# A 31-tap depthwise convolution: four taps in one stationary tile of 32 columns

## The chip, the core and the metric

The kernel runs on one core of a Trainium2 chip. The metric is the time of one execution on the device in microseconds (us); each number below is from one of three timed runs or from one execution taken by the hardware profiler. TensorE (PE) does the matmuls, VectorE (DVE), ScalarE (ACT) and GpSimd (POOL) the elementwise work, and SyncE's queue (SP) issues nearly all DMA transfers, in order.

## The reference

The reference is a two-layer transformer over 1024 latent and 256 context tokens with 1024 channels, in fp32. The change is in layer 0, a Conformer convolution module:

```python
u = h @ w_pw1 + b_pw1
a, g = jnp.split(u, 2, axis=-1)
v = a * jax.nn.sigmoid(g)
v = dwconv(v, w_dw, b_dw)          # 31 taps along the tokens, each channel with its own weights
v = jax.nn.silu(layernorm(v, ln_g, ln_b))
return v @ w_pw2 + b_pw2
```

After it come a gated feed-forward layer, a layer of windowed attention and a second feed-forward layer, which take most of the time and are not touched.

## The kernel before

Channels lie on the 128 partitions, in eight chunks; tokens lie along the free dimension. For chunk c the gated product fills a row `v` of 1325 columns: 512 + 512 latent and 256 context tokens, with 15 zeros before, between and after. The convolution makes 1295 output columns from it, each a sum over 31 shifted reads of `v`.

The eight chunks are computed in rounds (the loop over c in the block under `manual_schedule`). There the order on PE, DVE, ACT and POOL is that of the code; the SP queue's order is set by a scheduler. In round c the convolution of chunk c runs beside the first product of chunk c+1. Each weight is split into two parts, so `glu_mm` does 24 matmuls for one half (gate or value) of one of three token tiles, 0 and 1 of 512 columns, 2 of 256. Its two PSUM tiles rotate (`s`, two buffers). `glu_out` applies the sigmoid on ACT and writes its part of `v` on DVE. Beside that, `ada_steps` computes a block of modulation values in four parts on PE, each with its own 512 KB of weights, loaded through the two buffers `raw`, which the weights of the product (`wh`, `wl`) pass through as well.

The 31 taps of a chunk are shared out by `NPE` and `NDV` (L816, L817): in chunks 0 to 5, TensorE takes 2 (`tap_steps`: a diagonal 128x128 stationary matrix for each tap, then three copies by ACT and one addition by POOL), DVE takes 18, multiplying and adding into an accumulator `cacc` that lies in PSUM (`dve`), and ACT and POOL take 11 together: ACT multiplies (`first` and `prod`), POOL adds into `a2`. Chunk 6 has 4, 17 and 10, chunk 7 has 10, 14 and 7. At the end of a chunk `last` adds both accumulators into `y`, and `ymean` sums `y` over channels on TensorE. Chunk 7 has no next product beside it; the layer norm follows it.

## Time and profile before

| what | value |
| --- | --- |
| three timed runs | 2763.06, 2765.3 (median), 2769.14 us |
| the profiled execution: time, span | 2764.74 us, 2762.8 us |
| busy share of the span: PE, DVE, ACT, POOL | 96%, 62%, 37%, 22% |
| mean granted TensorE clock | 0.991 of full speed |

The span runs from the first to the last instruction; the profiled execution's own time is 1.94 us longer than it. A share of the whole span says little of one stage. The convolution and what prepares it take the first 400 us; the rounds run from about 82 to 399 us.

### The profile page before, as it was taken

The page shows a single profiled execution, that of the slowest core. Times are in us where ns is not written, and L with a number is a line of the kernel's source. Part 1 is how long each engine was busy: PE and PEld are TensorE (multiplying, and loading weights), DVE is VectorE, ACT ScalarE, POOL GpSimd, SP SyncE. Part 2 cuts the span into 40 slices and gives each one's busy share as a digit, 9 for nine tenths or more (in the row PEclk, how much of TensorE's full clock was granted, in tenths as well). Part 3 has the DMA queues.
Part 4 walks back from the last instruction along what each step waited for, and adds up shares of the span by engine and source line. Part 5 has one row for each costly group of instructions (what it writes and reads, how often), then busy time and mean ns, then how long its engine had stood idle before and what let it go on. Part 6 is the DMA issues. An engine that isn't in the chain of part 4 may idle for free.

```text
span 2762.8 us, 32879 instructions
## 1 busy us (share of the span) xinstructions
PE 2654.9 (96%) x13280; PEld 2151.3 (78%) x13280; DVE 1707.3 (62%) x2325; ACT 1011.8 (37%) x1430; POOL 613.0 (22%) x423
## 2 busy tenths in 40 slices
PE   5999989999999999999999998999999999999997
PEld 3766645778888888888887887888878888888886
DVE  6899965554454554454547758999865545555546
ACT  5554535552111122111123427777652222222223
POOL 1788853320000000000003205566420000000003
PEclk9999999999999999999999999999999999999998
DMA  6222355321111111111111451232111111111111
GB/s 234 69 77 84 103 199 186 114 78 68 39 38 39 39 39 39 38 39 39 39 39 46 151 183 45 73 81 53 39 54 50 50 46 49 51 46 46 52 48 69
DMA packets 62759, 198.23 MB, mean 72 GB/s; under 512 B 7696, under 2 KB 13456, under 8 KB 60304
## 3 DMA queue, kind: packets, MB, share of 16 engines
q1 hardware_dynamic: 62608, 196.14, 20.9%
q8 instruction: 104, 1.70, 0.3%
q14 instruction: 47, 0.39, 0.0%
HBM read 180.38 MB, written 15.73 MB: 71 GB/s over the span
## 4 chain that ended last, share of the span: by engine, by line
PE 78%; DVE 12%; ACT 5%; issue 2%; POOL 1%; DMA 1%; SPq 0%; DVEq 0%; ACTq 0%; POOLq 0%
PE up_ps L186 38%; PE dn_ps L186 18%; PE glu_ps L186 4%; DVE cacc L740 3%; PE wo_ps L186 3%; PE pw_ps L186 2%; PE pB L186 2%; PE pA L186 2%; PE tp L1419 1%; DVE tl L175 1%; DVE wl L128 1%; PE v_ps L186 1%; PE ada_ps L204 1%; PE dn_tail L186 1%; DVE mx L1397 1%
## 5 line engine op out<-in xcount | busy, mean ns | idle before, releaser
L128 DVE TENSOR_TENSOR wl<-raw,wh 128x1024 fp32r<-128x1024 f32 x181 | 237.7, 1317 | 515.9 <-issue 312.1
L186 PE MATMUL up_ps<-x_l,wh 128*128 128x512 f32 (+1 forms) x1760 | 415.0, 370 | 4.2 <-POOL x_l L315 4.2
L186 PE MATMUL up_ps<-x_h,wl 128*128 128x512 f32 (+1 forms) x1760 | 409.7, 369 | 0.2 <-ACT x_h L304 0.2
L186 PE MATMUL up_ps<-x_h,wh 128*128 128x512 f32 (+1 forms) x1760 | 407.9, 369 | 0.0
L250 POOL TENSOR_TENSOR acc<-acc,scrh 128x256 f32<-128x256 f32 (+1 forms) x36 | 37.4, 1039 | 1575.2 <-ACT scrh L249 1573.3
L186 PEld LDWEIGHTS up_ps<-x_l,wh 128*128 128x128 f32 x1760 | 311.9, 189 | 64.2 <-POOL x_l L315 5.8
L186 PEld LDWEIGHTS up_ps<-x_h,wh 128*128 128x128 f32 x1760 | 311.4, 189 | 55.8 <-issue 0.8
L186 PEld LDWEIGHTS up_ps<-x_h,wl 128*128 128x128 f32 x1760 | 310.5, 189 | 56.2 <-issue 0.8
L454 DVE SCALAR_TENSOR_TENSOR y<-dn_ps,mods,y 128x512 f32<-128x512 f32 (+1 forms) x400 | 270.3, 694 | 129.1 <-PE dn_ps L186 129.0
L126 ACT CAST wh<-raw 128x1024 fp32r<-128x1024 f32 x194 | 201.9, 1042 | 358.2 <-PE dn_ps L186 328.1
L409 ACT ACTIVATE c<-up_ps,pv 128x1282 f32<-128x1282 f32 (+1 forms) x88 | 115.6, 1315 | 588.3 <-PE up_ps L186 588.3
L746 POOL TENSOR_TENSOR a<-a,pr 128x1295 f32<-128x1295 f32 x75 | 223.9, 2985 | 60.6 <-ACT pr L745 50.7
L186 PE MATMUL dn_ps<-gl,wh 128*128 128x512 f32 (+1 forms) x800 | 232.7, 372 | 0.7 <-DVE y L454 0.7
L186 PE MATMUL dn_ps<-gh,wl 128*128 128x512 f32 (+1 forms) x800 | 231.5, 371 | 0.0
L186 PE MATMUL dn_ps<-gh,wh 128*128 128x512 f32 (+1 forms) x800 | 231.0, 370 | 0.0
L740 DVE SCALAR_TENSOR_TENSOR cacc<-v,pv,cacc 128x1295 f32<-128x1295 f32 x131 | 205.7, 1570 | 4.0
L1413 POOL TENSOR_TENSOR p<-p,rd 128x640 f32<-128x640 f32 (+1 forms) x128 | 154.4, 1237 | 234.1 <-DVE rd L1411 164.9
L413 DVE SCALAR_TENSOR_TENSOR c<-up_ps,pv,c 128x1281 f32<-128x1281 f32 (+1 forms) x88 | 124.6, 1416 | 121.6 <-ACT c L409 121.6
L186 PEld LDWEIGHTS dn_ps<-gl,wh 128*128 128x128 f32 x800 | 142.7, 188 | 31.7 <-DVE y L454 6.5
L186 PEld LDWEIGHTS dn_ps<-gh,wh 128*128 128x128 f32 x800 | 145.1, 188 | 27.1
L186 PEld LDWEIGHTS dn_ps<-gh,wl 128*128 128x128 f32 x800 | 145.0, 188 | 26.9
L745 ACT ACTIVATE pr<-v,pv 128x1295 f32<-128x1295 f32 x75 | 102.9, 1377 | 73.5 <-POOL a L746 58.6
(252 smaller groups left out, 4088.4 us busy)
## 6 DMA issues: line engine op xcount, KB each, us to landing
raw<-in_up_dram SPq DMA_DIRECT2D x88, 512.0 KB, 3.5
ada<-in_adaw_dram SPq DMA_DIRECT2D x11, 2048.0 KB, 8.5
raw<-in_down_dram SPq DMA_DIRECT2D x44, 512.0 KB, 3.5
raw<-in_adaw_dram SPq DMA_DIRECT2D x38, 512.0 KB, 3.9
raw<-in_pw_dram SPq DMA_DIRECT2D x32, 512.0 KB, 3.6
qs<-q_dram SPq DMA_DIRECT2D x32, 256.0 KB, 5.3
raw<-in_wo_dram SPq DMA_DIRECT2D x16, 512.0 KB, 3.5
ada<-in_adaw_dram SPq DMA_DIRECT2D x7, 1024.0 KB, 13.6
```

Of the source, the lines that this page charges most:

```text
L126: nc.scalar.copy(out=wh, in_=raw)
L128: lo_engine[0].tensor_sub(out=wl, in0=raw, in1=wh)
L175: (leng or nc.vector).tensor_sub(out=l_out, in0=src, in1=h_out)
L186: nc.tensor.matmul(ps, lhsT=w, rhs=x, start=first and n == 0, stop=last and n == len(seq) - 1)
L250: (eng or nc.gpsimd).tensor_add(out=acc, in0=acc, in1=sq)
L409: nc.scalar.activation(out=c, in_=ps[:, :W], func=AF.Identity, bias=seg("fdb", l * 2 * NJ + ab * NJ + j, 1), scale=wd[1])
L413: nc.vector.scalar_tensor_tensor(out=c[:, 1:W], in0=ps[:, 0:W - 1], scalar=wd[0], in1=c[:, 1:W], op0=ALU.mult, op1=ALU.add)
L454: nc.vector.scalar_tensor_tensor(out=h, in0=ps[:, m * n:(m + 1) * n], scalar=mod(l, 5, dc, s), in1=h, op0=ALU.mult, op1=ALU.add)
L740: nc.vector.scalar_tensor_tensor(out=r.acc, in0=v[:, j:j + OW], scalar=tap(j), in1=r.acc, op0=ALU.mult, op1=ALU.add)
L745: nc.scalar.activation(out=pr, in_=v[:, j:j + OW], func=AF.Copy, scale=tap(j))
L746: nc.gpsimd.tensor_tensor(out=r.a2, in0=r.a2, in1=pr, op=ALU.add)
L1413: nc.gpsimd.tensor_tensor(out=it.p4[:, hh, :it.wid], in0=it.p4[:, hh, :it.wid], in1=rd[:, hh:hh + 1].to_broadcast([P, it.wid]), op=ALU.mult)
```

## The change

TensorE's taps in a chunk become 8 (chunks 0 to 5), 16 and 28, those of DVE 13, 8 and 0, those of ACT and POOL 10, 7 and 3. One stationary tile now holds four taps of 32 channels: its 128 rows are four copies of these channels' `v`, each copy shifted by m columns against the one before (m is a quarter of TensorE's taps), and its 32 columns are the 32 channels. Four such tiles beside each other, g = 0 to 3, cover the 128 channels and write the four quarters of the partitions. With m steps along the columns that gives 4m taps. The matmuls write `cacc` itself, and DVE adds its taps onto it; the copies by ACT and the addition by POOL of the old path are gone.

The shifted copies are made by DMA: `Shifted.load(t)` issues 16 transfers from `v` (4 shifts by 4 groups, 32 partitions each), once for each token tile, 48 in a chunk. In front of the rounds the code creates `Shifted(0, ...)` and calls `load(0)` twice. The weights are brought in by 16 small transfers (`load_taps`) into the buffer `vp`, which the shifted copies use afterwards, and are put in order by 32 copies on ACT (`pack_taps`). `a2` has one buffer instead of two. The parts of the modulation block and the product's weights are loaded at other places, and the matmuls of token tile 2 take `wl` first.

The diff, cut to its core (the lines that it removes are those of `tap_diags`, `tap_steps` and the old loop above):

```diff
+NPE = (8, 8, 8, 8, 8, 8, 16, 28)
+NDV = (13, 13, 13, 13, 13, 13, 8, 0)
...
+    def mm3(ps, ops, by_chunk=False, first=True, last=True, wl_first=False):
+        if wl_first:
+            seq = [(wl, xh) for wh, wl, xh, xl in ops]
+            seq += [(wh, xl) for wh, wl, xh, xl in ops]
+            seq += [(wh, xh) for wh, wl, xh, xl in ops]
...
+        id4 = cv.tile([P, 32], F32, name="id4", bufs=1)
+        nc.vector.tensor_reduce(out=id4, in_=ident.rearrange("p (r m) -> p m r", m=32),
+                                axis=AX.X, op=ALU.add)
+        wpk = cv.tile([P, SUM_M, 4], F32, name="wpk", bufs=1)
+        def load_taps():
+            o, n = SEG["wdw"]
+            w = cv.tile([P, 4, n], F32, tag="vp", name="wdw4", bufs=1)
+            for r in range(4):
+                for g in range(4):
+                    nc.sync.dma_start(out=w[32 * r:32 * r + 32, g],
+                                      in_=par[32 * g:32 * g + 32, o:o + n])
+            return w
+        def pack_taps(w):
+            for r in range(4):
+                rows = slice(32 * r, 32 * r + 32)
+                for c in range(KC):
+                    m = NPE[c] // 4
+                    o = sum(NPE[:c]) // 4
+                    nc.scalar.copy(
+                        out=wpk[rows, o:o + m, :],
+                        in_=w[rows, :, c * TAPS + m * r:c * TAPS + m * r + m].rearrange("p g s -> p s g"))
...
+        M = [n // 4 for n in NPE]
+        MO = [sum(M[:c]) for c in range(KC)]
+        def tap_weights(c):
+            m = M[c]
+            if m * P <= 256:
+                w = cv.tile([P, 256], F32, tag="dg", name="dg", bufs=1)
+            else:
+                w = cv.tile([P, OW], F32, tag="pr", name="dg", bufs=2)
+            w = w[:, :m * P]
+            nc.gpsimd.tensor_tensor(
+                out=w.rearrange("p (g m) -> p g m", m=32),
+                in0=id4.unsqueeze(1).to_broadcast([P, 4 * m, 32]),
+                in1=wpk[:, MO[c]:MO[c] + m, :].rearrange("p s g -> p (s g)").unsqueeze(2).to_broadcast([P, 4 * m, 32]),
+                op=ALU.mult)
+            return w
+        class Shifted:
+            def __init__(self, c, v):
+                self.v, self.m = v, M[c]
+                self.sp = OW + self.m - 1 - 512
+                self.a = cv.tile([P, 4, OW - 512 + 12], F32, tag="vp", name="vp", bufs=1)
+                self.b = [nt.tile([P, 512], F32, tag=("acc", "acc", "nt", "nt")[g], name="vpb",
+                                  bufs=(2, 2, 3, 3)[g]) for g in range(4)]
+            def copy(self, dst, c0, c1):
+                for r in range(4):
+                    for g in range(4):
+                        x0 = self.m * r + c0
+                        nc.sync.dma_start(out=dst(g)[32 * r:32 * r + 32],
+                                          in_=self.v[32 * g:32 * g + 32, x0:x0 + c1 - c0])
+            def load(self, t):
+                e = self.sp + self.m - 1
+                f = min(512, PADW + 512 - 3 * self.m)
+                if t == 0:
+                    self.copy(lambda g: self.a[:, g, 0:f], 0, f)
+                elif t == 1:
+                    self.copy(lambda g: self.a[:, g, f:e], f, e)
+                else:
+                    self.copy(lambda g: self.b[g], self.sp, self.sp + 512)
+            def rows(self, g, s, o, n):
+                if o < self.sp:
+                    return self.a[:, g, o + s:o + s + n]
+                return self.b[g][:, o - self.sp + s:o - self.sp + s + n]
+        def pe_taps(c, vp, w):
+            r = {}
+            sp = vp.sp
+            def part(o, e):
+                if o == 0:
+                    r["acc"] = pc.tile([P, 1536], F32, tag="cv", name="cacc")[:, :OW]
+                for s in range(vp.m):
+                    for g in range(4):
+                        nc.tensor.matmul(r["acc"][32 * g:32 * g + 32, o:e],
+                                         lhsT=w[:, (4 * s + g) * 32:(4 * s + g + 1) * 32],
+                                         rhs=vp.rows(g, s, o, e - o), start=s == 0,
+                                         stop=s == vp.m - 1)
+            return r, [lambda o=o, e=e: part(o, e)
+                       for o, e in ((0, 512), (512, sp), (sp, 1024), (1024, OW))]
+        def conv_steps(c, v, r, npe, ndve):
...
+                r["a2"] = cv.tile([P, OW], F32, tag="a2", name="a2", bufs=1)
+                nc.scalar.activation(out=r["a2"], in_=v[:, npe + ndve:npe + ndve + OW],
+                                     func=AF.Identity, bias=seg("bdw", c, 1), scale=tap(npe + ndve))
...
+                nc.gpsimd.tensor_tensor(out=r["a2"], in0=r["a2"], in1=pr, op=ALU.add)
...
+            dq = [lambda j=j: dve(j) for j in range(npe, npe + ndve)]
...
+            w4 = load_taps()
...
             apply(1, 0, 2)
             glu_out(q, 0)
+            vp = Shifted(0, q.v)
+            vp.load(0)
             apply(1, 2, 4)
             bcast_b(2)
+            pack_taps(w4)
+            dgs = tap_weights(0)
+            vp = Shifted(0, q.v)
+            vp.load(0)
             glu_mm(q, 1, 0, 0)
             normalize_h(2)
...
             glu_mm(q, 1, 1, 1)
             glu_out(q, 1)
+            vp.load(1)
             glu_mm(q, 2, 0)
             glu_mm(q, 2, 1)
             glu_out(q, 2)
+            vp.load(2)
...
+            ld_ada(0, 0)
+            ld_ada(0, 1)
             for c in range(KC):
+                wide_taps = M[c] * P > 256
+                if wide_taps:
+                    dgs = tap_weights(c)
+                r, taps = pe_taps(c, vp, dgs)
+                first, pq, dq, last = conv_steps(c, q.v, r, NPE[c], NDV[c])
                 ada_ps = pc.tile([P, 512], F32, tag="s", name="ada_ps", bufs=2) if c == KC - 1 else None
+                ada = ada_steps(0, 4 + c, lambda u, c=c: araw[c, u], ada_ps)
                 first()
                 run(pq, 1)
                 if c + 1 < KC:
                     q = glu_begin(c + 1)
                     glu_mm(q, 0, 0)
                     run(ada, 1)
+                    ld_ada(c, 2)
+                    run(pq, 0 if wide_taps else 1)
+                    glu_mm(q, 0, 1)
+                    run(ada, 1)
+                    ld_ada(c, 3)
+                    run(taps, 4)
+                    glu_out(q, 0)
+                    vp = Shifted(c + 1, q.v)
+                    vp.load(0)
+                    run(pq, 1)
                     if c > 0:
                         ymean(c - 1)
+                    glu_mm(q, 1, 0)
                     run(ada, 1)
+                    w_load()
+                    run(dq, 3)
                     run(pq, 2)
+                    run(ada, 1)
+                    w_load()
+                    glu_mm(q, 1, 1)
+                    run(ada, 1)
                     run(dq, 3)
                     run(pq, 1)
                     glu_out(q, 1)
+                    vp.load(1)
+                    if M[c + 1] * P <= 256:
+                        dgs = tap_weights(c + 1)
+                    wh = w_hi()
                     glu_mm(q, 2, 0)
                     run(ada, 1)
+                    run(dq, 2)
+                    run(pq, 1)
+                    w_lo(wh)
+                    ld_ada(c + 1, 0)
+                    wh = w_hi()
                     glu_mm(q, 2, 1)
                     run(dq, 1)
                     glu_out(q, 2)
+                    vp.load(2)
+                    w_lo(wh)
+                    ld_ada(c + 1, 1)
                     run(pq, 99)
                     run(dq, 99)
                 else:
+                    run(ada, 1)
+                    ld_ada(c, 2)
+                    run(ada, 1)
+                    ld_ada(c, 3)
+                    run(pq, 99)
                     ymean(c - 1)
+                    run(taps, 2)
                     run(ada, 2)
+                    run(taps, 1)
+                    run(ada, 1)
+                    for i in range(4):
+                        load_ada(i)
+                    run(taps, 1)
+                    run(dq, 99)
                 last()
```

On the SP queue, this is what stood between the last loads ahead of the rounds and the second round (`raw` from `in_adaw` is a part of the modulation block, from `in_pw` a weight of the product):

```order
L626 DMA ada_128<-in_adaw_dram 128x2048 x2
L599 DMA h_112<-in_hT_dram 128x8x256
L106 DMA raw<-in_pw_dram 128x1024 x2
L106 DMA raw<-in_adaw_dram 128x1024 x4
L106 DMA raw<-in_pw_dram 128x1024 x2
L106 DMA raw<-in_adaw_dram 128x1024 x4
```

In its place there stands, from the tap weights to the second round:

```order
L631 DMA wdw_244<-in_par_dram 32x248 x16
L109 DMA raw<-in_pw_dram 128x1024 x2
L778 DMA vp<-v 32x512 x32
L778 DMA vp<-v 32x273 x16
L778 DMA vpb<-v 32x512 x16
L109 DMA raw<-in_adaw_dram 128x1024 x4
L778 DMA vp<-v 32x512 x16
L109 DMA raw<-in_pw_dram 128x1024 x2
L778 DMA vp<-v 32x273 x16
L109 DMA raw<-in_adaw_dram 128x1024
L778 DMA vpb<-v 32x512 x16
L109 DMA raw<-in_adaw_dram 128x1024 x3
```

Between the loads of `raw` now stand bursts of 16 transfers; the first part of a modulation block is behind the second burst of a chunk, the second part behind the third (`vpb`).

On PE, from the last matmuls of chunk 0's product, through the taps of round 0 (`tap_ps`), to the first part of the modulation block (`glu_ps` is the product of the next chunk):

```order
L186 MATMUL glu_ps<-xh_508,wh 128x256 x8
L756 MATMUL tap_ps<-v,dg 128x512 x4
L756 MATMUL tap_ps<-v,dg 128x271 x2
L186 MATMUL glu_ps<-xl_242,wh 128x512 x8
L186 MATMUL glu_ps<-xh_241,wl 128x512 x8
L186 MATMUL glu_ps<-xh_241,wh 128x512 x8
L204 MATMUL ada_ps<-raw,c_80 32x512 x2
```

and now, from the start of round 0's product to the end of its taps (`cacc`):

```order
L193 MATMUL glu_ps<-xl_262,wh 128x512 x8
L193 MATMUL glu_ps<-xh_261,wl 128x512 x8
L193 MATMUL glu_ps<-xh_261,wh 128x512 x8
L211 MATMUL ada_ps<-raw,c_80 32x512 x2
L193 MATMUL glu_ps<-xl_262,wh 128x512 x8
L193 MATMUL glu_ps<-xh_261,wl 128x512 x8
L193 MATMUL glu_ps<-xh_261,wh 128x512 x8
L211 MATMUL ada_ps<-raw,c_80 32x512 x2
L806 MATMUL cacc<-vp,dg 32x512 x8
L806 MATMUL cacc<-vp,dg 32x272 x8
L806 MATMUL cacc<-vpb,dg 32x240 x8
L806 MATMUL cacc<-vpb,dg 32x271 x8
```

The taps have moved from ahead of the round's product to behind its first token tile and the second part of the modulation block; 6 matmuls of 128 columns each have become 32 of 32 columns.

## Rows read from the trace of the kernel before

**Rows 1.** The page, part 1: busy us, share of the span, instructions.

```profile
PE 2654.9 (96%) x13280; PEld 2151.3 (78%) x13280; DVE 1707.3 (62%) x2325; ACT 1011.8 (37%) x1430; POOL 613.0 (22%) x423
```

**Rows 2.** Stretches of two rounds: length, busy us by engine, clock, DMA share, GB/s.

```profile
126.15:166.00 39.85, 35.54 (x173) 25.31 (x172) 39.25 (x32) 18.93 (x19) 32.94 (x16) 0.98 0.28 91
166.00:207.00 41.00, 40.56 (x195) 29.62 (x194) 35.75 (x26) 21.86 (x22) 35.30 (x18) 0.98 0.20 67
```

**Rows 3.** The timeline of DVE: start, us, instruction, idle before and its releaser.

```profile
112.59 0.75 DVE L709 SCALAR_TENSOR_TENSOR v<-glu_ps,pv,sg 128x512 f32<-128x512 f32 x1 [3.26 <-PE glu_ps L186]
...
118.78 0.48 DVE L709 SCALAR_TENSOR_TENSOR v<-glu_ps,pv,sg 128x256 f32<-128x256 f32 x1 [0.57 <-PE glu_ps L186]
...
322.38 0.47 DVE L709 SCALAR_TENSOR_TENSOR v<-glu_ps,pv,sg 128x256 f32<-128x256 f32 x1
...
361.51 0.48 DVE L709 SCALAR_TENSOR_TENSOR v<-glu_ps,pv,sg 128x256 f32<-128x256 f32 x1 [1.57 <-PE glu_ps L186]
...
397.10 1.62 DVE L767 TENSOR_TENSOR y<-cacc,a 128x512 f32<-128x512 f32 x3 [8.81 <-POOL a L761]
```

**Rows 4.** The timeline of PE in round 0, same columns.

```profile
81.74 3.60 PE L756 MATMUL tap_ps<-v,dg 128*128 128x512 f32 x8
...
86.66 2.21 PE L186 MATMUL glu_ps<-xl,wh 128*128 128x512 f32 x8
...
92.44 1.05 PE L204 MATMUL ada_ps<-raw,c 128*32 128x512 f32 x4
93.42 2.12 PE L186 MATMUL glu_ps<-xl,wh 128*128 128x512 f32 x8
...
106.74 2.12 PE L186 MATMUL glu_ps<-xl,wh 128*128 128x512 f32 x8
...
112.32 1.11 PE L186 MATMUL glu_ps<-xl,wh 128*128 128x256 f32 x8
...
118.51 3.60 PE L756 MATMUL tap_ps<-v,dg 128*128 128x512 f32 x8
```

**Rows 5.** The tile cacc: instructions, ns min/median/max, first and last start.

```profile
L740 DVE SCALAR_TENSOR_TENSOR cacc<-v,pv,cacc x131: 1558/1572/1574, 86.3 to 386.7; 128x1295 f32<-128x1295 f32 x131
L767 DVE TENSOR_TENSOR y<-cacc,a x24: 406/675/691, 126.1 to 398.3; 128x512 f32<-128x512 f32 x16, 128x256 f32<-128x256 f32 x8
```

**Rows 6.** The tile pr: the additions on POOL, same columns.

```profile
L746 POOL TENSOR_TENSOR a<-a,pr x75: 2924/2995/3041, 85.4 to 391.1; 128x1295 f32<-128x1295 f32 x75
```

**Rows 7.** The timeline of PE: a modulation block ahead of the rounds.

```profile
31.71 2.00 PE L204 MATMUL ada_ps<-ada,c 128*32 128x512 f32 x16
```

**Rows 8.** The timeline of ACT, and of PE (last row), ahead of the rounds.

```profile
3.71 0.22 ACT L86 ACTIVATE c<-ctile 128x16 f32<-128x16 f32 x1
...
64.17 1.51 ACT L665 ACTIVATE xh<-h,mods,amul 128x512 fp32r<-128x512 f32 x2
...
75.17 0.66 ACT L707 ACTIVATE sg<-glu_ps,pv 128x512 f32<-128x512 f32 x1
...
75.89 1.21 PE L186 MATMUL glu_ps<-xl,wh 128*128 128x256 f32 x8 [0.53 <-ACT sg L707]
```

**Rows 9.** The timeline of SP in the attention layer: issues of small transfers.

```profile
1609.39 0.42 SPq L1320 DMA_DIRECT2D ks<-k_dram  x1
...
1612.64 0.42 SPq L1319 DMA_DIRECT2D ks<-k_dram  x1
```

**Rows 10.** The page, part 6: DMA issues, KB each, median us to landing.

```profile
raw<-in_adaw_dram SPq DMA_DIRECT2D x38, 512.0 KB, 3.9
...
ks<-k_dram SPq DMA_DIRECT2D x32, 112.0 KB, 4.5
ks<-k_dram SPq DMA_DIRECT2D x32, 80.0 KB, 2.2
```

**Rows 11.** The timeline of PE after a wait ahead of the rounds.

```profile
41.44 1.12 PE L216 MATMUL ada_pt<-ident,ada_sb 128*128 128x128 f32 x4 [7.74 <-ACT ada_sb L210]
...
43.21 0.63 PE L186 MATMUL glu_ps<-xh,wh 128*128 128x512 f32 x1
43.63 0.63 PE L186 MATMUL glu_ps<-xh,wl 128*128 128x512 f32 x1
```

More of the change, by code (lines that the diff above doesn't have):

```diff
@@ L34 @@
 DEPTH = 2
+NPE = (8, 8, 8, 8, 8, 8, 16, 28)
+NDV = (13, 13, 13, 13, 13, 13, 8, 0)
+SUM_M = sum(NPE) // 4
 SEGS = [
@@ L701, in glu_mm @@
                 ops = ops[4 * part:4 * part + 4]
-            mm3(q.ps[half][:, :n], ops, part is not None, part in (None, 0), part in (None, 1))
+            mm3(q.ps[half][:, :n], ops, part is not None, part in (None, 0), part in (None, 1),
+                t == 2)
         def glu_out(q, t):
@@ L765, in last @@
             def last():
                 for t, (o, n) in enumerate(TOK):
[L767 to L768 removed]
+                    nc.vector.tensor_tensor(out=ys[t][:, c, :], in0=r["acc"][:, OOF[t]:OOF[t] + n],
+                                            in1=r["a2"][:, OOF[t]:OOF[t] + n], op=ALU.add)
             pq = [lambda j=j: prod(j) for j in range(npe + ndve + 1, TAPS)]
[L771 removed]
@@ L772, in conv_steps @@
-            return first, tap_steps, pq, dq, last
+            dq = [lambda j=j: dve(j) for j in range(npe, npe + ndve)]
+            return first, pq, dq, last
         def ymean(c):
@@ L870, in hybrid_dit_kernel, with ld_ada, w_load, w_hi @@
             ys = [make_h(t, "y") for t in range(3)]
-            for c in range(KC):
-                first, tap_steps, pq, dq, last = conv_steps(c, q.v, dgs, NPE[c], NDV[c])
+            araw = {}
+            wraw = []
+            def ld_ada(c, u):
+                if c < KC:
+                    araw[c, u] = load_raw(adaw[0, 4 + c, :, 2 * u:2 * u + 2, :])
+            def w_load():
+                wraw.append(load_raw(queue[len(loaded) + len(wraw)][1]))
+            def w_hi():
+                wh = wpool.tile([P, 1024], F32R, tag="wh", name="wh", bufs=3)
+                nc.scalar.copy(out=wh, in_=wraw[0])
+                return wh
+            def w_lo(wh):
+                wl = wpool.tile([P, 1024], F32R, tag="wl", name="wl")
+                nc.vector.tensor_sub(out=wl, in0=wraw.pop(0), in1=wh)
+                loaded.append((wh, wl))
+            ld_ada(0, 0)
+            ld_ada(0, 1)
+            for c in range(KC):
+                wide_taps = M[c] * P > 256
[3 more added lines that the diff above has]
+                first, pq, dq, last = conv_steps(c, q.v, r, NPE[c], NDV[c])
                 ada_ps = pc.tile([P, 512], F32, tag="s", name="ada_ps", bufs=2) if c == KC - 1 else None
-                ada = ada_steps(0, 4 + c, None, ada_ps)
+                ada = ada_steps(0, 4 + c, lambda u, c=c: araw[c, u], ada_ps)
                 first()
-                run(dq, 1)
                 run(pq, 1)
                 if c + 1 < KC:
-                    parts, add = tap_steps("pr")
-                    for f in parts:
-                        f()()
-                    add()
                     q = glu_begin(c + 1)
@@ L931, in hybrid_dit_kernel @@
-                    assert not pq and not dq
-                    for f in evs:
-                        f()
-                    add()
+                    run(taps, 1)
[4 more added lines that the diff above has]
+                    run(dq, 99)
                 last()
```

72 lines of the change are left out of this document (4 added, 68 removed).

## The prediction

> **What bounds the kernel now.** I read the page's busy table first, then stretches of the rounds, then DVE's and PE's timelines in one round. TensorE is busy for 96% of the span [rows 1], but the change touches only the convolution, so the stage decides. In two successive rounds, of 39.85 and 41.00 us, DVE is busy for 39.25 and 35.75 us and PE for 35.54 and 40.56 us [rows 2]: neither has room, and the end passes from one to the other. A round is read between the writes of the last third of `v`: 118.78 to 322.38 is five rounds, 40.7 us each; round 6 takes 39.1 us (to 361.51); chunk 7 ends with its `y` at 398.72, 37.2 us later, 8.8 us of which DVE waited for POOL [rows 3].
>
> Within round 0, PE's taps take 4.9 us (81.74 to 86.66) and the product and the modulation block 31.85 us (86.66 to 118.51); a half product of 512 columns takes 5.8 us, a part of the modulation block 0.98 us (92.44 to 93.42), and from the end of token tile 1 to the end of tile 2 it is 6.2 us (112.32 to 118.51) [rows 4]. Ahead of the rounds ACT is in one chain: token tile 2's product waits at 75.89 for the sigmoid that ACT starts at 75.17, behind all its normalising work [rows 8].
>
> **The change, part by part.**
>
> *DVE and POOL.* DVE loses five of 18 taps of 1.57 us, 7.9 us a round; 13 remain, 20.4 us, and the sums into `y` (1.76 us) [rows 5]. With the writes of `v` (0.75, 0.75 and 0.48 us [rows 3]) DVE has 24.2 us a round beside the weight splits. POOL keeps nine additions of 3.0 us, 27 us [rows 6]. So neither bounds a round near 40 us any more. `a2` has one buffer, so ACT's next `first` waits for `last`, and the sigmoid of tile 0 stands behind it; both are done before TensorE needs that PSUM tile, behind the taps. If that cover went, each us would be a us of the round.
>
> *TensorE's taps.* An fp32 matmul is two instructions in the trace (the 8 instructions at 81.74 are 4 matmuls in the order). A modulation block ahead of the rounds, 8 matmuls of 512 columns that go to four column groups in turn, takes 2.00 us [rows 7], so four beside each other take 1.00 us. That is the shape of the new taps. Two steps of 1295 columns come to 2 x 1295 / 1024 x 2.00 = 5.1 us, against 4.9 before: eight taps for the price of two. With m = 4 it is 10.1 us, with m = 7 17.7 us. The bounds: nothing below this, since column groups are all that overlaps here; above, four times as long if they did not overlap. I take the row, since its shape is the same. The Trainium skill ("TensorE: Matmul & The Clock Gate", Measured speedup vs the span model) gives less for packing: 3.07 times for four tiles. From the 0.9 us of a matmul at 81.74 that would be an estimated 1.17 us for four instead of 1.00 and put about 10 us on the sum; the row of this kernel is faster than the page.
>
> A round of TensorE without waits is then 31.85 + 5.1 + about 1.0 for the three column means (like one part of the block) = 37.9 us, less than the 40.7 us of now.
>
> *The bursts on SP.* Each chunk adds 48 transfers to one queue. Small transfers on 32 partitions were issued seven in 3.25 us, 0.464 us apart [rows 9], so a burst of 16 takes 7.4 us. No row has a transfer from SBUF to SBUF; the nearest are those of 80 KB, which land in 2.2 us, against 4.5 us for 112 KB; a `raw` of 512 KB takes 3.9 us [rows 10]. Lower bound of a burst: 16 issues at 0.41 us (the issue alone, without the gap) = 6.6 us. Upper: eight in flight that take 4.5 us to land, 9.0 us. I take 7.4, the pitch of the same kind of transfer.
>
> In a round the second and third burst stand ahead of the modulation block's first two loads, which the PE order needs behind the product's halves for tile 0. From the end of tile 1's product (0): `v` is written 1.0 us later (112.32 to 113.34 [rows 3, 4]), the burst ends at 8.4, part 0 lands at 12.3, where PE needs it at 6.2 + 5.8 = 12.0. The next burst runs from 8.9 to 16.3; its `v` is there in time, after PE's 6.2 and some 2 us of DVE. Part 1 lands at 20.2, PE needs it at 12.0 + 1.0 + 5.6 (a half as at 106.74 to 112.32) = 18.6. So PE waits 1.6 us, and the round is 37.9 + 1.6 = 39.5 us: five rounds save 5 x 1.2 = 6 us. Round 6 has 5.1 us of taps more, 44.6 against 39.1: it loses 5.5 us. In chunk 7 no product lies in between: part 1 lands 14.0 us behind the end of its product (20.2 - 6.2), then follow 1.0 + 1.0 + 10.8 of taps (789 of 1295 columns) + 1.0 + 6.9 + 1.8 of sums = 36.5 us against 37.5: a gain of 1 us, though POOL's wait of 8.8 us is gone.
>
> *Ahead of the rounds.* `pack_taps` puts 32 copies into ACT's chain. The shortest ACT row with few columns takes 0.22 us [rows 8]; I take 0.2 us, 6.4 us in all (bounds: 0 if they overlap wholly, 7.0 at 0.22). The chain holds PE, so the rounds start 6.4 us late, at 88.1 instead of 81.74. The shifted copies use the buffer of the packed weights, so the first burst starts behind the copies, at 64.2 + 6.4 = 70.6. `load(0)` is issued twice and the second waits until the first has landed: 78.0, 80.2, 87.6. Then the bursts for tiles 1 and 2, to 102.4, and behind them part 0 of the first modulation block, which lands at 106.3. TensorE stands before it at 88.1 + 5.8 = 93.9: a wait of 12.4 us. From there round 0 takes 26.1 us (92.44 to 118.51) and 5.1 of taps, and it ends at 137.5. After a wait of 7.7 us, PE's matmuls came 0.42 us apart (43.21, 43.63) instead of 0.24 [rows 4, 11]; I add 1 us for that. Round 0 ends 20 us later than at 118.51.
>
> **Sum.** +20 - 6 + 5.5 - 1 = +18.5 us on the profiled execution's 2764.7 us, which lies 0.6 us below the median of the runs. Predicted: 2784 us, 0.7% slower. The rest of the kernel is as before. A change under 0.2%, 5.5 us, can't be told from none here.
>
> **Rivals.**
> - *A, faster: SP's bursts never hold TensorE.* For it: the DMA engines are busy for only 0.20 to 0.28 of the time in the rounds [rows 2], and a burst of 6.6 us would bring part 1 in time. Then rounds are 37.9 us (-14), round 6 +4, chunk 7 about -11 (26.5 us), and only the copies remain ahead, +6.5: 2750 us. It decides from bursts below 6.6 us in the rounds and, for round 0, below 4.3 us (93.9 - 3.9 - 2.2 - 70.6, over four), which no row supports.
> - *B, no change: the rounds run at TensorE's pace, but round 0 is held as reckoned.* +20 - 14 + 4 - 11 = -1: 2764 us. It needs 0.41 us an issue, 12% less than the row.
> - *C, slower still: the transfers land late.* With 9.0 us a burst: 4 x 1.6 + 2.3 = +9 ahead, 3.2 us in each of six rounds, 3 in chunk 7, 31 us more: 2815 us. For it: 112 KB on 32 partitions took 4.5 us, and reads and writes now both go to SBUF; against it: 80 KB took 2.2.
> - *D: the column groups don't overlap, so the change doesn't do what it says.* 23 steps in all x 1295 / 512 x (3.6 - 1.0) = +151 us: some 2930 us. Rows 7 speak against it.
>
> **How the numbers follow.** The forecast 50%, A 10%, B 14%, C 22%, D 4%. Faster by over 0.2% is A and a little more: 0.11. Within 0.2% is B and the forecast's lower edge: 0.16. Slower: 0.73. The range reaches from between A and B, 2757, to a little above C, 2818; the forecast's own range is 2774 to 2795.
>
> **What would show it.** PE waiting for a DMA into `raw` ahead of the modulation block's parts: some 12 us in round 0 and 1 to 2 us in each later round. SP issues of `vp` 0.46 us apart. 32 copies on ACT in 6 to 7 us. `cacc` matmuls 5 us a chunk. Rounds of 39 to 40 us, `y` of chunk 7 some 19 us later than 398.7. I am wrong if the first round's wait is under 5 us, if the taps take much over 6 us, or if a round is still bound by DVE's or POOL's chain.

## The result, and the profile after

The changed kernel takes 2840.2 us (median of four runs, 2834.2 to 2844.7) against 2765.5 us for the kernel before beside it: a ratio of 1.0268, 95% interval 1.0245 to 1.0290. It is slower, as forecast, but by 75 us and not by 19: the time lies outside the range of 2757 to 2818. The profiled execution took 2839.65 us (span 2837.9).

The first part of the page answers to [rows 1]: busy us, share of the span, instructions.

```profile
PE 2660.7 (94%) x13860; PEld 2166.6 (76%) x13860; DVE 1624.5 (57%) x2273; ACT 987.0 (35%) x1425; POOL 549.3 (19%) x384
```

VectorE and GpSimd lost 83 and 64 us of work, as the edit says, and TensorE is as busy as before. What grew is the part of the span in which TensorE is idle, from 108 to 177 us. The windows of the changed kernel, cut at the writes of the last third of `v`, show where (columns as in [rows 2]; the first row is round 0, then rounds 1, 2, 3 and 6 and chunk 7).

```profile
86.30:153.60 67.30, 42.33 (x242) 30.49 (x241) 21.94 (x18) 17.66 (x16) 26.82 (x13) 0.82 0.36 101
153.60:198.20 44.60, 38.45 (x236) 29.35 (x235) 29.35 (x25) 17.54 (x16) 28.46 (x14) 0.96 0.45 131
198.20:243.10 44.90, 39.65 (x236) 30.22 (x235) 29.25 (x25) 17.55 (x16) 28.50 (x14) 0.92 0.47 130
243.10:291.10 48.00, 39.26 (x236) 29.28 (x235) 29.03 (x24) 17.46 (x16) 28.25 (x14) 0.93 0.42 122
...
384.40:430.90 46.50, 39.70 (x287) 31.18 (x285) 27.10 (x23) 13.51 (x13) 22.34 (x12) 0.97 0.67 214
430.90:469.20 38.30, 23.30 (x262) 10.64 (x266) 5.89 (x10) 4.69 (x4) 7.49 (x3) 0.73 0.64 224
```

Rounds 1 to 5 (153.6 to 384.4) take 46.2 us each; before they took 40.7 [rows 3]. In such a round VectorE is busy for 29 us where it was 36 to 39 [rows 2], and nobody else has more to do than TensorE's 38 to 40: the round waits. The view of waits names for what (PE, 60 to 480 us: us in total, times, longest).

```profile
PE ada_ps L211 <- DMA raw<-in_adaw_dram: 70.6, 15, 22.7
PE glu_ps L193 <- DVE wl L964: 11.9, 6, 2.3
```

Here `wl` is the low part of a weight, which VectorE makes (`w_lo`) when ACT has cast the high part (`w_hi`). In the kernel before, PE's largest item in that stretch was 11.1 us in all, for ACT's evacuation `tp` of the taps. Round 2 on PE's timeline (start, us, instruction, idle before and its releaser), which answers to [rows 4]:

```profile
198.81 1.97 PE L193 MATMUL glu_ps<-xh,wh 128*128 128x512 f32 x8
203.65 1.92 PE L211 MATMUL ada_ps<-raw,c 128*32 128x512 f32 x4 [2.87 <-DMA raw<-in_adaw_dram]
205.50 3.78 PE L193 MATMUL glu_ps<-xl,wh 128*128 128x512 f32 x8
...
213.54 0.62 PE L211 MATMUL ada_ps<-raw,c 128*32 128x512 f32 x2 [0.37 <-DMA raw<-in_adaw_dram]
...
237.75 2.00 PE L193 MATMUL glu_ps<-xl,wh 128*128 128x512 f32 x8
241.76 2.11 PE L193 MATMUL glu_ps<-xh,wl 128*128 128x512 f32 x8 [2.01 <-DVE wl L964]
```

Behind the wait at 203.65 the same four and eight instructions take 1.92 and 3.78 us in place of 1.05 and 2.12: the granted clock of 203.2 to 208.2 is 0.50, the lower of its two levels. This wait is paid for twice. Not every wait is: behind the 2.01 us at 241.76 the eight take 2.11 us, at a clock of 1.00.

On SP's timeline, the chain of round 0 and one round:

```profile
67.00 32.97 SPq L778 DMA_DIRECT2D vp<-v  x48
100.08 10.05 SPq L778 DMA_DIRECT2D vpb<-v  x16
110.23 1.03 SPq L109 DMA_DIRECT2D raw<-in_adaw_dram  x2
...
198.23 0.53 SPq L109 DMA_DIRECT2D raw<-in_adaw_dram  x1
198.86 10.24 SPq L778 DMA_DIRECT2D vpb<-v  x16
209.22 5.75 SPq L109 DMA_DIRECT2D raw<-in_adaw_dram  x3
217.32 10.86 SPq L778 DMA_DIRECT2D vp<-v  x16
```

Four bursts end 43.1 us after 67.00, and one takes 10.0 to 11.2 us in rounds 0 to 5, where the prediction had 7.4 and nothing over 9.0. The view of line 778 (copies: ns min/median/max of an issue) and then the page's sixth part (KB, median us to landing) tell issue from transfer:

```profile
L778 SPq DMA_DIRECT2D vp<-v x272: 507/589/1545, 67.0 to 432.0; - x136
```

```profile
vp<-v SPq DMA_DIRECT2D x128, 64.0 KB, 2.0
```

The copies land in 2.0 us, like the 80 KB transfers of [rows 10]; it is their issue that takes 0.59 us, 0.63 with the gap, and not the 0.42 of [rows 9].

### The profile page after: what moved, and what is told of

Its sections match the earlier page's. It is cut to its first block, busy times and chain, and to the rows that moved or that the text cites. A ratio compares the mean times of both kernels' runs of the same rounds, so it can differ in the third digit from the quotient of the medians.

```text
span 2837.9 us, 34480 instructions
## 1 busy us (share of the span) xinstructions
PE 2660.7 (94%) x13860; PEld 2166.6 (76%) x13860; DVE 1624.5 (57%) x2273; ACT 987.0 (35%) x1425; POOL 549.3 (19%) x384
## 4 chain that ended last, share of the span: by engine, by line
PE 76%; DVE 9%; ACT 5%; SPq 3%; DMA 3%; issue 2%; POOL 1%; DVEq 0%; ACTq 0%; POOLq 0%
PE up_ps L193 37%; PE dn_ps L193 17%; PE glu_ps L193 4%; SPq L778 3%; PE wo_ps L193 2%; DMA raw<-in_adaw_dram 2%; PE pw_ps L193 2%; PE cacc L806 2%; PE pB L193 2%; PE pA L193 2%; DVE tl L178 1%; PE tp L1525 1%; PE ada_ps L211 1%; DVE mx L1503 1%; PE v_ps L193 1%
## 5 line engine op out<-in xcount | busy, mean ns | idle before, releaser
L131 DVE TENSOR_TENSOR wl<-raw,wh 128x1024 fp32r<-128x1024 f32 x167 | 207.2, 1241 | 516.2 <-issue 312.6
L129 ACT CAST wh<-raw 128x1024 fp32r<-128x1024 f32 x180 | 187.5, 1043 | 358.1 <-PE dn_ps L193 328.1
L833 POOL TENSOR_TENSOR a<-a,pr 128x1295 f32<-128x1295 f32 x62 | 189.7, 3060 | 168.7 <-ACT pr L832 166.6
L420 DVE SCALAR_TENSOR_TENSOR c<-up_ps,pv,c 128x1281 f32<-128x1281 f32 (+1 forms) x88 | 124.6, 1416 | 121.7 <-ACT c L416 121.7
L193 PEld LDWEIGHTS dn_ps<-gl,wh 128*128 128x128 f32 x800 | 142.7, 188 | 31.8 <-DVE y L461 6.4
L827 DVE SCALAR_TENSOR_TENSOR cacc<-v,pv,cacc 128x1295 f32<-128x1295 f32 x86 | 135.0, 1569 | 47.2 <-PE cacc L806 45.1
L424 DVE SCALAR_TENSOR_TENSOR c<-up_ps,pv,c 128x1281 f32<-128x1281 f32 (+1 forms) x88 | 124.5, 1416 | 2.3
```

Of the source, the lines that this page charges most:

```text
L129: nc.scalar.copy(out=wh, in_=raw)
L131: lo_engine[0].tensor_sub(out=wl, in0=raw, in1=wh)
L193: nc.tensor.matmul(ps, lhsT=w, rhs=x, start=first and n == 0, stop=last and n == len(seq) - 1)
L420: nc.vector.scalar_tensor_tensor(out=c[:, 1:W], in0=ps[:, 0:W - 1], scalar=wd[0], in1=c[:, 1:W], op0=ALU.mult, op1=ALU.add)
L424: nc.vector.scalar_tensor_tensor(out=c[:, 0:W - 1], in0=ps[:, 1:W], scalar=wd[2], in1=c[:, 0:W - 1], op0=ALU.mult, op1=ALU.add)
L827: nc.vector.scalar_tensor_tensor(out=acc, in0=v[:, j:j + OW], scalar=tap(j), in1=acc, op0=ALU.mult, op1=ALU.add)
```

## The experiments

All but two were run once, beside a run of the kernel before on the same chip (2763 to 2767 us). Round: mean of rounds 1 to 5 between the writes of the last third of `v`. Raw: PE's waits for `raw` from 60 to 480 us.

| kernel | us | round | raw |
|---|---|---|---|
| before | 2765.5 | 40.7 | none |
| changed | 2840.2 | 46.2 | 70.6 |
| x1_one_load | 2831.2 | 46.8 | 62.2 |
| x2_act_raw | 2816.4 | 44.4 | 15.4 |
| x4_two_queues | 2835.8 | 48.0 | 15.7 |
| x5_raw_free | 2773.3 | 40.4 | 13.0 |
| x6_raw_wl | 2772.6 | 40.0 | 15.6 |
| x7_pack | 2771.4 | 40.6 | 17.3 |
| x9_hbm | 2759.2 | 38.6 | 9.5 |
| x10_hbm_pack | 2761.0 | 39.2 | 10.1 |
| x11_m1 | 2770.3 | 41.4 | 15.5 |
| x12_hbm_only | 2826.6 | 46.9 | 59.2 |
| x13_mid | 2809.1 | 44.2 | 58.5 |
| x14_twelve | 2807.3 | 42.6 | 49.4 |
| x15_eight | 2776.2 | 39.2 | 23.0 |

My theory was that the burst's length on SP, ahead of the two raw loads, sets the round; the rivals were that the order on SP does so whatever the length, that the transfers themselves are slow, and that a second chain (VectorE's sum, ScalarE's `first`, the sigmoid) is as long.

**x1_one_load** leaves out the first of the two equal loads of chunk 0.

```diff
-            vp = Shifted(0, q.v)
-            vp.load(0)
             apply(1, 2, 4)
```

> The first of the two calls of load(0) ahead of the rounds is left out; its data is written again by the second. Theory (the issues on SP, 0.63 us apart, set the path): part 0 of the first modulation block lands 16 x 0.63 + 2.0 = 12 us earlier, TensorE's wait in round 0 falls from 22.7 to about 11 us, the rounds after it stay at 46 us, the time falls by 12 us to 2828. Rival (DVE and ACT hold round 0): the wait falls but round 0 ends as before, 2838 to 2842.

9 us less and not 12. PE's wait in round 0 falls from 22.7 to 14.8 us, and the round, which begins 3.9 us sooner, takes 58.0 in place of 67.3 us: its end comes 13.2 us sooner, and rounds 1 to 6 give 5.7 of that back.

**x3_probe** is the kernel before with bursts of copies between scratch tiles at its start, which change no result (its time of 2837.2 us holds them).

```diff
+        for r, g in rg:
+            sy.dma_start(out=d[q(r), g], in_=s[q(g), 2 * r:2 * r + 512])
+        for r, g in rg:
+            sy.dma_start(out=d[q(r), g, 0:128], in_=s[q(g), 2 * r:2 * r + 128])
...
+        for r, g in rg:
+            sy.dma_start(out=d[q(r), g], in_=m[q(g), 2 * r:2 * r + 512])
```

> The kernel before, with bursts of copies of scratch data put ahead of everything, so its own time is longer by their length and says nothing else. Forms on SP: (1) SBUF to SBUF, 32 partitions x 512, as in the change; (2) the same x 128 columns; (3) within the same partitions; (4) 128 partitions; (5) SBUF to HBM; (6) HBM to SBUF; (7) HBM to SBUF with 4 x 512 for each of 32 partitions; then (8) form 1 from ACT's queue. Theory (the issue of a copy with both ends in SBUF costs more): forms 1 to 3 0.6 us apart whatever the columns, 5 and 6 0.4 to 0.47. Rival (bytes): form 2 much closer together than form 1.

Here `s` and `d` are in SBUF and `m` in HBM. One issue by line (min/median/max ns): SBUF to SBUF with 512 columns, with 128, and on 128 partitions; then SBUF to HBM, HBM to SBUF, and SBUF to SBUF on ACT's queue.

```profile
L74 SPq DMA_DIRECT2D prd<-prs x16: 507/590/611, 2.3 to 15.2; - x16
...
L76 SPq DMA_DIRECT2D prd<-prs x16: 588/589/590, 15.8 to 25.3; - x16
...
L80 SPq DMA_DIRECT2D prd<-prs x8: 524/582/615, 36.2 to 40.7; - x8
...
L82 SPq DMA_DIRECT2D prm<-prs x8: 418/423/587, 41.3 to 44.7; - x8
...
L84 SPq DMA_DIRECT2D prd<-prm x16: 309/420/431, 45.2 to 52.5; - x16
...
L88 ACTq DMA_DIRECT2D prd<-prs x16: 513/602/903, 61.4 to 73.5; - x16
```

With both ends in SBUF an issue takes 0.59 us for a quarter of the bytes and for four times the partitions alike; with one end in HBM 0.42 (0.30 for loads of 256 KB, L86). The theory holds, the rival falls: the row I had taken the pitch from, `ks<-k_dram`, was another kind of transfer, and the burst is bound by issues, not by bytes.

**x2_act_raw** leaves the raw loads where they stand in the program, but ACT issues parts 0 and 1.

```diff
...
-                    araw[c, u] = load_raw(adaw[0, 4 + c, :, 2 * u:2 * u + 2, :])
+                    araw[c, u] = load_raw(adaw[0, 4 + c, :, 2 * u:2 * u + 2, :],
+                                          nc.scalar if u < 2 else nc.sync)
```

> Only parts 0 and 1 of each modulation block are issued from ACT's queue instead of behind the bursts on SP; the bursts and their number stay. Theory: TensorE no longer waits for a DMA into raw; what is next are the late weight split on DVE (2.2 us a round) and the last burst, rounds of 40 to 42 us, round 0 shorter by 10 to 14 us, chunk 7 by 8 us or more; 2775 to 2795 in all. Rival (the transfers and the memory they share are slow, or DVE's, ACT's and POOL's chain holds the rounds): rounds stay at 44 us or more, 2820 to 2840.

Neither: the waits for raw in the rounds are gone, but another came. ACT's issue waits for VectorE's w_lo, and the cast and the sigmoid that PE needs stand behind it. ACT and PE in round 2:

```profile
185.97 0.34 ACTq L109 DMA_DIRECT2D raw<-in_adaw_dram  x1
186.40 1.04 ACT L960 CAST wh<-raw 128x1024 fp32r<-128x1024 f32 x1 [7.83 <-DVE wl L965]
187.36 0.47 ACT L739 ACTIVATE sg<-glu_ps,pv 128x256 f32<-128x256 f32 x1
...
187.88 2.50 PE L193 MATMUL glu_ps<-xl,wh 128*128 128x512 f32 x5 [5.64 <-ACT sg L739]
```

**x4_two_queues** has one load and gives half of each burst to ACT.

```diff
-                        nc.sync.dma_start(out=dst(g)[32 * r:32 * r + 32],
+                        (nc.sync, nc.scalar)[r % 2].dma_start(out=dst(g)[32 * r:32 * r + 32],
...
```

> One load(0), and every second group of four copies is issued from ACT's queue: the same transfers and bytes, half the issues on SP. Theory (issue): a burst takes 5 us on SP, part 1 lands about 16 us behind tile 1's product, before TensorE needs it, rounds of 40 to 42 us; 2775 to 2800 (ACT pays 24 issues a round). Rival (the transfers themselves take 0.63 us each on the DMA engines): the bursts land as late as before, rounds stay at 45 to 46 us, 2825 to 2835.

The burst on SP halves (8 copies in 4.98 us at 231.15), which again speaks for issue and against bytes, but ACT spends 5.30 us on the other half there, ahead of its cast and sigmoid, and PE waits 34.6 us for the sigmoid. The time, just above the rival's span, says nothing on the theory, since this wait is new.

**x5_raw_free** issues parts 0 and 1 on ACT too, but behind the sigmoid and at the end of the round (with one load).

```diff
...
                     glu_out(q, 2)
+                    ld_ada(c + 1, 0)
                     vp.load(2)
                     w_lo(wh)
-                    ld_ada(c + 1, 1)
                     run(pq, 99)
+                    ld_ada(c + 1, 1)
```

> As the changed kernel with the first of the two equal loads of chunk 0 left out (2831 us measured for that alone), and with the first two parts of each modulation block issued by the ACT queue after the sigmoid of the 256 columns and at the end of the round, where nothing that PE waits for stands behind them. Theory (the 10 us burst on SP stands ahead of these two loads and so ends each round): PE's waits for raw fall from 62 us to under 20, the rounds go from 46 us to 41 to 43 (the wait for w_lo stays), and the time to 2795 to 2810. Rival (the second chain, the sums of DVE, then ACT's first product, two more products, the sigmoid, is as long): PE waits for raw no more, but the rounds stay at 45 us or above and the time at 2820 or above.

58 us less than x1_one_load, more than expected: rounds of 40.4 us, and waits for raw of 13.0 us. All 48 copies still take their 0.63 us or more each; they just stand ahead of nothing urgent. The rival of a second chain falls.

**x6_raw_wl** adds w_lo of the first block right behind `v` of tile 1, and **x7_pack** moves the packing behind the weight casts as well.

```diff
...
+                    w_lo(wh)
                     run(ada, 1)
                     run(dq, 2)
                     run(pq, 1)
-                    w_lo(wh)
```

> As the run before it, and w_lo of the first weight block stands in DVE's order right behind v of tile 1, ahead of the reduction of the modulation block and of two taps. Theory: PE's wait for wl (11.9 us in 6 stretches in the changed kernel) goes, the rounds come to 39.5 to 41 us as the prediction had them, and the time to 2780 to 2795. Rival (DVE only waits elsewhere, for ACT's cast of w_hi, and the taps that stood in the gap come later): within 5 us of the run before it.

> As x6_raw_wl, and the 32 packing copies on ACT stand behind the sigmoid and the two weight casts of chunk 0 (the filter rows lie in another buffer, so that the first burst no longer waits for the packing). Theory (the packing's 4.0 us stand on the path that sets v of tile 1): the first v of 256 columns comes 3 to 5 us sooner and the time is 3 to 6 us under that of x6_raw_wl. Rival (what is late in round 0 is SP's chain of bursts, so that what the front gains is lost there): within 2 us of x6_raw_wl.

Both rivals hold. The wait for w_lo (9.9 us in x5) goes, and the time moves by 1 us: PE waits 8.0 us ahead of the taps instead, which start as VectorE's sums into `y` end (at 259.53, behind 259.43). With the packing late the rounds start 7.5 us sooner (79.57 for 87.11), and the time moves by 1 us again. Where these gains go is taken up under *What stays open*.

**x9_hbm** is x6_raw_wl with tiles 0 and 1 copied by way of HBM; **x12_hbm_only** does only that, on x1_one_load.

```diff
+                if t < 2:
+                    nc.sync.dma_start(out=self.vd[:, lo:hi], in_=self.v[:, lo:hi])
...
-                    self.copy(lambda g: self.a[:, g, 0:f], 0, f)
+                    self.copy4(self.a[:, :, 0:f], 0, f)
```

> As x6_raw_wl, but the shifted copies of tiles 0 and 1 take the way through HBM: one store of v's new columns, then four loads of 32 partitions by four groups, 5 issues where there were 16. Theory (with the two raw loads off SP its bursts end nothing any more in rounds 1 to 5): the rounds stay within 1 us of those of x6_raw_wl, and only round 0, where three bursts follow each other, gets 5 to 15 us shorter; time 2770 to 2785. Rival (SP's bursts still set the round, over the weight loads behind them): the rounds get 2 us shorter or more, time under 2770. Other rival: the way through HBM lands so late that the taps wait for it and the time is over that of x6_raw_wl.

> As the changed kernel with the first load left out (2831 us), and only the way of the copies of tiles 0 and 1 changed: one store of v's new columns to HBM and four loads, 5 issues in place of 16. The two raw loads still stand behind the bursts on SP. It asks whether the length of the bursts in front of the raw loads is what decides, as against their order. Theory (length): the first raw load comes some 6 us sooner after v of tile 1 and is hidden, the second still waits for the full burst of tile 2; PE's waits for raw fall from 62 us to 20 to 40, the rounds to 41 to 44 us, time 2785 to 2810. Rival (the one burst of tile 2 ahead of the second raw load sets the round by itself): PE's waits stay over 50 us, time 2820 or above.

x9_hbm is 13 us faster than x6_raw_wl: 7 us of it are in rounds 1 to 5 (38.6 for 40.0), 4 in chunk 7. The time is the first rival's; the rounds lie between the theory (within 1 us) and that rival (2 us or more), so that SP still set them is not shown. In its round at 205 PE is busy 37.8 of 38.0 us:

```profile
205.00:243.00 38.00, 37.84 (x236) 27.43 (x235) 28.95 (x24) 17.52 (x16) 29.36 (x14) 1.00 0.60 168
```

In x12 the rival holds. SP, then PE:

```profile
183.71 0.35 SPq L109 DMA_DIRECT2D raw<-in_adaw_dram  x1
185.59 10.01 SPq L779 DMA_DIRECT2D vpb<-v  x16
195.71 1.02 SPq L109 DMA_DIRECT2D raw<-in_adaw_dram  x2
```

```profile
193.97 1.98 PE L193 MATMUL glu_ps<-xh,wh 128*128 128x512 f32 x8
199.80 1.07 PE L211 MATMUL ada_ps<-raw,c 128*32 128x512 f32 x2 [3.86 <-DMA raw<-in_adaw_dram]
```

Part 0 comes in time now, and PE waits for part 1 instead: behind `v` at 185.08 stand the burst of 10 us and a landing of 4.1, and the round is that chain, whether part 0 was late or not. Of two waits in a round the later one decides, and here only the last burst counts.

**x10_hbm_pack** is x9_hbm with x7's packing, and **x11_m1** gives TensorE 4 taps in place of 8 there and VectorE's three more a place in its order (12 and 11 runs).

```diff
-NPE = (8, 8, 8, 8, 8, 8, 16, 28)
-NDV = (13, 13, 13, 13, 13, 13, 8, 0)
+NPE = (4, 4, 4, 4, 4, 4, 16, 28)
+NDV = (16, 16, 16, 16, 16, 16, 8, 0)
...
```

> All that helped together: one load, raw loads off SP, w_lo early, copies of tiles 0 and 1 by way of HBM (2759.2 us measured with these), and the packing behind the weight casts. Theory (the packing's 4 us are on the path ahead of the rounds, and round 0 of the HBM version is no longer held by SP, so that the gain is kept): 2752 to 2757. Rival (as in x7_pack, what the front gains of 7 us is given back in the rounds): 2758 to 2760.

> As x10_hbm_pack, but in chunks 0 to 5 TensorE takes 4 taps and not 8, VectorE 16 and not 13, and the sum of ScalarE's products one more. PE is busy 37.7 of 38.0 us in such a round of the HBM version; four taps less take 2.2 us from it, VectorE goes from 28.9 to 33.6 us and GpSimd from 29.4 to 32.3. Theory (PE is what bounds these rounds): 1 to 2 us a round less, 2742 to 2751. Rival (VectorE idles 8 us a round where no tap can be put, waiting for TensorE's taps and for v, so the added taps make the sum late, and with it ScalarE's first product and the sigmoid): the rounds get longer, 2756 or above.

x10 is faster than the kernel before by 5 us: ratio 0.9977 (0.9968 to 0.9986). It lies in neither span, next to the rival's, and the packing gives nothing on top of x9. x11 is slower than both, 1.0018 (1.0010 to 1.0027) against before, as its rival had it: VectorE's sum ends later, then `first`, two products and the sigmoid, and rounds are 41.4 us. With eight taps the split is not too high.

**x13_mid** keeps all on SP, but puts the raw loads behind the eighth copy of the bursts (one load, w_lo early).

```diff
...
                 for r in range(4):
+                    if r == 2 and mid:
+                        mid()
...
```

> As the changed kernel with the first load left out (2831 us), w_lo early, and nothing on another queue: all 48 copies of a chunk and all raw loads stay on SP at the old pitch, but the two raw loads of the next chunk stand in the middle of the bursts of tiles 1 and 2, behind the eighth copy (chunk 0's own two loads stay behind its bursts). It asks whether it is the place in SP's order that decides, and not the number or length of the copies, nor that another queue issues. Theory (the place): PE's waits for raw in rounds 1 to 5 fall to a few us, these rounds go from 45 to 49 us to 39 to 42, round 0 stays at 50 to 58, time 2780 to 2797. Rival (SP is simply too full: the copies that now stand behind the raw loads come late and the taps wait for them instead): rounds over 43 us, time 2810 or above.

22 us gained, not 34 to 51. In rounds 1 to 5 PE waits 25.3 us for raw, against 23.9 in x1, and not at all for w_lo, against 10.7. What went is the wait for w_lo, which this run moves too; what the place gave by itself is not shown. The rounds of 44.2 us are in the rival's span, but what PE waits for is the raw load, not the copies. SP, then PE, in round 3:

```profile
231.52 5.97 SPq L780 DMA_DIRECT2D vpb<-v  x8
237.60 0.52 SPq L109 DMA_DIRECT2D raw<-in_adaw_dram  x1
238.16 6.05 SPq L780 DMA_DIRECT2D vpb<-v  x8
```

```profile
236.11 1.98 PE L193 MATMUL glu_ps<-xh,wh 128*128 128x512 f32 x8
243.73 1.07 PE L211 MATMUL ada_ps<-raw,c 128*32 128x512 f32 x2 [5.65 <-DMA raw<-in_adaw_dram]
```

Part 1 lands 6.1 us after its issue with eight copies behind it, 13.0 us after `v` at 230.66; PE wants it some 7 us after `v`. Half a burst is still too much ahead of it.

**x14_twelve and x15_eight** settle the length. Order, queue, bytes, both loads and what waits for what are those of the changed kernel; pairs of copies are one transfer on 64 partitions, which carries 64 neighbouring channels at one shift, so the taps' sums are not the reference's. In x15 the pairs are (0, 2) and (2, 4).

```diff
-                for r in range(4):
+                for r, e in ((0, 1), (1, 2), (2, 4)):
...
```

> The changed kernel, with both loads of chunk 0 and its whole order, but each burst in 12 issues instead of 16: the copies for the third and fourth row group are one transfer on 64 partitions. The bytes are the same; those transfers carry channels that the taps should not get, so the sums of the taps are not the reference's. At 0.63 us an issue a burst takes 7.6 us, which is what the prediction had reckoned with (7.4). Theory (the size of the burst is the step that failed): the rounds come to 40 to 43 us, the prediction's 39.5 and part of the 2 us of the wait for w_lo that it had not seen, and the time to 2785 to 2805. Rival (a burst of 7.6 us ahead of the raw loads still holds the rounds as much, since TensorE's clock falls after any wait): rounds of 45 us and a time of 2822 or more.

> As x14_twelve with 8 issues a burst, all on 64 partitions (the taps again get other channels' columns, with the same bytes): 5.1 us a burst. After v of tile 2 the second raw load is then issued at 5.6 us and lands at 10, where TensorE needs it at about 10. Theory (size): the rounds come to 39 to 41 us, only the wait for w_lo is left in them, round 0 to 45 to 50, the time to 2762 to 2782. Rival: as before, any burst ahead of the raw loads costs; 2800 or more.

A burst of each, x14 then x15:

```profile
183.74 7.54 SPq L779 DMA_DIRECT2D vpb<-v  x12
```

```profile
171.63 4.94 SPq L779 DMA_DIRECT2D vpb<-v  x8
```

Bursts of 10.2, 7.5 and 4.9 us give 2840, 2807 and 2776 us: 12 us of time for one of the burst. x14 is 2 us above the theory's span, its rounds of 42.6 us within it; x15 is within it. The rival falls; nor does the clock fall behind every wait (eight instructions take 2.14 us behind the 1.82 at 223.83 in x14).

## Why the prediction was wrong

*The step that failed* is the size of the bursts: "so a burst of 16 takes 7.4 us", with 9.0 as the upper bound. It is 10.0 to 11.2. The working itself said that no row had a transfer from SBUF to SBUF, and then took the issue of a load from HBM for its nearest kin and let only the landing vary; the landing was right at 2.0 us, the issue was not. The eight transfers in flight of its upper bound stand in no row. Rival C (2815) came nearest of all, for the wrong reason. The Trainium skill ("DMA: Bandwidth & Descriptors", Issuing engines are not separate DMA queues) holds the time that a queue takes to start a DMA to be usually small beside the DMA; here it is 0.59 against 2.0 us for one copy, but 10 against 2 for a burst, so the rule doesn't carry to many small copies on one queue. With the forecast's burst the kernel takes 2807 us (x14): of the miss of 56 us, 33 are this term, and 23 are not.

*A second reading was wrong*, and the burst hid it: that the `v` of the third burst "is there in time, after PE's 6.2 and some 2 us of DVE". In x14, with a burst as forecast, PE, then DVE:

```profile
171.83 1.12 PE L193 MATMUL glu_ps<-xh,wl 128*128 128x256 f32 x8
```

```profile
183.20 0.47 DVE L741 SCALAR_TENSOR_TENSOR v<-glu_ps,pv,sg 128x256 f32<-128x256 f32 x1
```

Tile 1's product ends at 171.83, and the third burst, at 183.74 above, waits for this `v`: 11.9 us behind it, where the prediction had 8.9. So PE still waits 2.7 us a round for raw in x14, where 1.6 was reckoned. With 1.8 us for w_lo, which was not reckoned, and 37.9 of work that is 42.4 of the round's 42.6 us; over five rounds these two are about 15 of the 23.

*Where the 56 us lie.* Round 0 ends at 153.6, not 138.8: 15. Of these 8 are the bursts: four take 43.1 us in place of 31.8, though they start 3.6 us sooner, and PE goes on at 114.60, not 106.3. Most of the rest is the `v` that ends the round, written 5.6 us behind its product and not 0.3. Five rounds of 46.2 for 39.5: 33. Round 6 and chunk 7 (46.5 for 44.6, 38.3 for 36.5): 4. Behind the convolution, 5, with the same work there; the other kernels vary by as much. The sign of the whole came out as forecast, that of a round did not: 1.2 us shorter was forecast, 5.5 longer was measured.

*The 6.7 us of a round.* PE's waits for raw are 5.2 us (26.1 in rounds 1 to 5) where 1.6 was reckoned: 3.6. The wait for w_lo is 1.9, and the prediction did not have it. What stands ahead of w_lo on VectorE:

```profile
231.83 0.75 DVE L741 SCALAR_TENSOR_TENSOR v<-glu_ps,pv,sg 128x512 f32<-128x512 f32 x1 [3.21 <-PE glu_ps L193]
235.07 0.19 DVE L226 TENSOR_REDUCE mods<-ada_pt 128x8 f32<-128x32 f32 x1 [2.49 <-PE ada_pt L223]
235.29 2.19 DVE L231 TENSOR_TENSOR mods<-mods,pv 128x8 f32<-128x8 f32 x1
237.41 3.17 DVE L827 SCALAR_TENSOR_TENSOR cacc<-v,pv,cacc 128x1295 f32<-128x1295 f32 x2
240.48 1.22 DVE L964 TENSOR_TENSOR wl<-raw,wh 128x1024 fp32r<-128x1024 f32 x1
```

A reduction that needs PE's transposes, its addition and two taps; each passes its delay on. I had priced VectorE as having room and had not followed its order. But the order alone would have been in time; the 1.9 us are the stretch of single instructions. This addition takes 2.19 us here, beside an addition of GpSimd, and 0.17 us in x12, where GpSimd is idle; in each of rounds 0 to 5 what it takes over 0.17 us, with what w_lo takes over 1.22 us, is PE's wait for w_lo to 0.01 us. In the two of x5's rounds 1 to 5 in which the addition takes 0.17 us PE does not wait for w_lo. The same stretch holds back the `v` of tile 2, which stands behind w_lo in VectorE's order. The remaining 1.2 us (by subtraction) is the lower clock behind the waits, for which I had 1 us in round 0 and none in the others: PE is busy 39.0 us a round and not 37.9, at a granted clock of 0.92 to 0.96. All three hang together: x5, which removes most of the waits for raw alone, brings the round to 40.4.

*What was right.* PE waits for the raw loads in round 0 and in each round, behind the bursts that the chain names. The taps cost what they should: in round 2 of x10, at the full clock, the 63 instructions of 171.17 to 176.70 are 5.5 us (5.1 forecast).

```profile
171.17 2.84 PE L817 MATMUL cacc<-vp,dg 128*32 128x512 f32 x32 [0.42 <-issue]
173.81 2.89 PE L817 MATMUL cacc<-vpb,dg 128*32 128x240 f32 x31
```

The Trainium skill's 3.07 times for four tiles ("TensorE: Matmul & The Clock Gate", Measured speedup vs the span model) would make it an estimated 5.9 us (2 x 1295 columns at 1.17 us for 512 in each of four); this trace is faster, and the measurement decides. The Trainium skill has that figure for tiles beside each other in rows of the array; in columns, as here, it has three tiles and 2.38 times. PE's floor of 37.9 us a round is reached in x9 (37.8 of 38.0). By their busy time VectorE and GpSimd bound nothing; where they meet, PE waits, as w_lo shows. The packing was over-priced, 3.98 us on ACT for 6.4 [rows 8]:

```profile
62.95 3.98 ACT L641 COPY wpk<-wdw 32x8 f32<-32x8 f32 x32
```

*What stays open.* x15 with both loads (2776 us) and x5 with one (2773 us) reach 39 to 40 us a round on different ways, but neither reaches x9's 38.6. The traces say what separates them. In x5, x6, x7, x9, x10 and x15 rounds 1 to 5 are of two kinds, with none between: 38.0 to 38.8 us where that addition takes under 0.5 us, and 40.4 to 42.0 where it takes 1.6 or more. x9 has one long round, x10 and x15 two, x5 and x6 three, x7 four. So x7 and x10 have one more than x6 and x9, which is 3 us of what they had gained ahead of the rounds. A round of each kind, in x15 (38.15 and 41.13 us):

```profile
203.18 0.45 DVE L231 TENSOR_TENSOR mods<-mods,pv 128x8 f32<-128x8 f32 x1
...
279.88 3.05 DVE L231 TENSOR_TENSOR mods<-mods,pv 128x8 f32<-128x8 f32 x1
```

No run moved this addition away from GpSimd's, so that it makes a round long is read from the order and not tested.

## What to carry to other kernels

Take the price of a DMA issue from a row with the same two ends, and where there is none, let the issue vary as well as the landing. Before adding transfers to an in-order queue, list what stands behind them and by when it is needed; moving two loads out from behind the copies was worth 58 us here (with one load of chunk 0), halving the copies' issues 64 (with both), and either turned a loss of 75 us into one of 6 to 11. Look also at the shortest and longest time of one instruction on an engine that has room: the same addition took 0.17 us or 3 here, and the rounds went with it. A load moved to another engine's queue must stand where its own wait blocks nothing: at the wrong place the same move gave 24 us and not 58.
